# The left-over-token loop between the loads and the products of the last expert half, and a final norm from row sums

## The chip, the core and the metric

The kernel runs on one core of one Trainium2 chip. The metric is device time in microseconds (us). Three runs of the kernel before took 2152.41, 2152.41 and 2153.8 us; their median is 2152.41 us. One further execution was profiled, and every row below comes from that one.

Names used here: PE is TensorE (PEld its weight loads), DVE is VectorE, ACT is ScalarE, POOL is GpSimd, SP is SyncE, which in this kernel mostly issues DMAs. All tensors are float32.

## What is computed

Two layers of a diffusion block over 256 latent tokens and 256 context tokens of width 1024. Each layer has three token mixers (attention, gated linear attention, neighbourhood attention) and then a mixture of experts. The second layer needs only the latent tokens behind its mixers, so its expert part has 256 tokens (two tiles of 128 rows) where the first layer's has 512 (four tiles). What this case touches is the end of each layer:

```
h2 = LN0(x) * (1 + scale2) + shift2
x  = LayerNorm(alpha * x + gate2 * HierMoE(h2))   # top-1 group, then top-2 experts in it

def layer_norm0(x):
    mu  = x.mean(-1)
    var = square(x - mu).mean(-1)
    return (x - mu) * rsqrt(var + 1e-6)
def layer_norm(x, g, b): return layer_norm0(x) * g + b

def expert_block(xb, e):          # blocks of 128 token slots, 32 experts
    return (silu(xb @ w1[e]) * (xb @ w3[e])) @ w2[e]      # 1024 -> 512 -> 1024
```

The next layer begins with `h = LN0(x) * (1 + scale1) + shift1` and one wide projection of h.

## The kernel before

**Experts.** `experts(l, T)` walks over "halves": pieces of 128 token slots that belong to one, two or four experts, 14 halves in layer 0 and 16 in layer 1. The last half of each layer holds two experts with 64 slots each. One expert's weights are six tiles of 1 MB: w1 (j = 0, 1), w3 (j = 2, 3), w2 (j = 4, 5). So a half of two experts needs eight tiles for `body` (the products h = x·w1 and x·w3, 32 matmuls in two PSUM tiles) and four for `tail` (the SwiGLU `act`, four transposes, and the products Y = act·w2 in two column halves of 512, each split into a high and a low part Yh and Yl for the exact scatter). `body(n)` runs ahead of `tail(n-1)`. After every second half, `combine` scatters the Y of two halves back to the token tiles: products `cb` with a selection matrix C, a multiplication with the gate row (`ct`, L1432), and an addition to x (L1433), on POOL or, for the second column half of the last pair, on DVE.

**Loads.** SP issues every weight load in program order (L1464 and, for halves of a tile, L1469). A load waits until the buffer that it will fill is free. The buffers are rings: `ew` with six tiles in both layers, `ewb`, and in layer 1 some `spare` tiles made of areas that the mixers had used. Once the rings are full, a load starts when the products on the tile that lay there are done.

**The loop.** Slots beyond what the halves hold are done by `overflow(l, T)`: a device loop `For_i` (L1546) over a number of blocks that is read from a tile at run time (`values_load`, L1545). With these inputs the number is zero; no instruction of the loop's body is in the trace. The loop stands behind the last `tail`. At a loop the five engines meet: each runs a short block of semaphore waits, branches, and goes on in the code behind the loop. Those waits are the EVENT_SEMAPHORE records of L1546.

**The final norm.** Before, it reads statistics with `bn_stats` (L336, one record for 512 columns) and `bn_aggr` (L338), makes the inverse root by a chain of ten short DVE instructions (L340 to L346) on several token tiles at once, and applies it. In layer 0 ACT scales (L1597), DVE multiplies with g (L1598), and POOL or DVE adds b (L1599); in layer 1 two DVE steps (L1590, L1593) do it, and SP stores the result (L1595). g and b (`lgb`) are two rows broadcast to 512 KB each (L1612).

**Layer 1's start.** Behind layer 0's loop come the loads of the modulation weights (`wmod`, 16 of 512 KB, L493), the products on them (`tmod`, L495), the store of two x tiles to memory (L1601), the norm that opens the layer (`norm_T`: statistics, `xh` on ACT at L539, transposes `hT` at L550), and the wide projection in exact three-pass products (L380 to L382).

**What sets the order.** Each engine runs its instructions in the order of the program, which the scheduler of the tile framework makes from the code's order with priorities; waits are semaphores between engines. DMAs are queued in the order in which SP or ACT issues them.

Of the kernel before, what the change touches and what calls it, by code (L numbers as in the profile page):

```python
# [10 lines left out]
F32 = mybir.dt.float32  # L11
# [238 lines left out]
class _Prog:  # L250
# [281 lines left out]
    def norm_T(self, l, xs):  # L532
# [3 lines left out]
        for a in range(0, 4, NT[l]):  # L536
            for t, (_, r, m) in enumerate(self.stats_all(xs[a:a + NT[l]], APN[l]), a):
                h = self.t([128, 1024], ("whi", "wlo")[t % 2] if l else "g4", name="xh")
                nc.scalar.activation(h, xs[t], AF.Identity, bias=m, scale=r)  # L539
                xh.append(h)  # L540
# [858 lines left out]
    def expert_tail(self, h1, h3, gate, w2, halves, end=False):  # L1399
# [20 lines left out]
    def combine(self, CY, T, last):  # L1420

        nc, mm = self.nc, self.nc.tensor.matmul
        for n in range(2):
            for t in range(T):
# [8 lines left out]
                (nc.vector if last and n else nc.gpsimd).tensor_tensor(self.x1[t][:, ns], self.x1[t][:, ns], tmp, op=ALU.add)  # L1433
# [10 lines left out]
    def load(self, l, us, n, js, step=2048, most=99, after=None):  # L1444
# [4 lines left out]
        for j in js:  # L1449
            for i in range(len(us)):  # L1450
# [7 lines left out]
                if n < 6 or n >= 6 + extra:  # L1458
# [4 lines left out]
                    for v in range(0, 2048, step):  # L1463
                        self.nc.sync.dma_start(x[:, v:v + step], src[:, v:v + step])  # L1464
# [7 lines left out]
    def experts(self, l, T):  # L1472
# [39 lines left out]
        def tail(dp, pr, us, hs):  # L1512
            end = SPL and 2 * dp + pr == len(halves) - 1
            self.load(l, us, 2 * dp + pr, (4,))
            self.load(l, us, 2 * dp + pr, (5,), 1024 if end else 2048)
            w = self.held[2 * dp + pr]
            Y = self.expert_tail(hs[0], hs[1], gates[dp][:, pr:pr + 1],
                                 lambda f, n, i: w[i, 4 + n][f], len(us), end)
# [8 lines left out]
        for n, x in enumerate(halves):  # L1527
            if x[1] == 1 and x[0] + 1 < len(gs):
                front(x[0] + 1)
            with self.later(0 if n else FIRST):  # L1530
                held[n] = body(*x)
            if n:
                tail(*halves[n - 1], held[n - 1])
        tail(*halves[-1], held[len(halves) - 1])
    def overflow(self, l, T):

# [4 lines left out]
        nc.vector.tensor_scalar(idx0, idx0, c["pcol"][:, 0:1], 6.0, op0=ALU.add, op1=ALU.mult)  # L1541
        if l:
            nc.vector.tensor_scalar(idx0, idx0, float(l * NE * 768), None, op0=ALU.add)
        table = self.a["ew"].rearrange("l e p j w -> (l e p j) w")
        nblk = nc.values_load(self.nblk[0:1, 0:1], min_val=0, max_val=16)  # L1545
        with self.tc.For_i(0, nblk, 1):  # L1546
# [3 lines left out]
            w = []  # L1550
            for j in range(6):
                ii = self.small(1, I32)
                nc.vector.tensor_scalar(ii, row, float(j), None, op0=ALU.add)
                x = self.t([128, 2048], "ew", name="ow")
                nc.gpsimd.indirect_dma_start(out=x, out_offset=None, in_=table, in_offset=bass.IndirectOffsetOnAxis(ap=ii[:, :1], axis=0))
                w.append(x)
# [10 lines left out]
            for m in range(2):  # L1567
                h = self.ps("h")
                for k in range(8):
                    mm(h, XT[:, k], w[2 * m + k // 4][:, 512 * (k % 4):512 * (k % 4) + 512], start=k == 0, stop=k == 7)  # L1570
                hs.append(h)
            Y = self.expert_tail(hs[0], hs[1], gate, lambda f, n, i: w[4 + n][:, 512 * f:512 * f + 512], 1)
            col = self.small(1)
            nc.vector.tensor_tensor(col, sel, c["pcol"][:, 0:1], op=ALU.add)
            self.combine([(self.spots(self.slot_rows(self.over, T), col, T),) + Y], T, False)
# [5 lines left out]
    def final_norm(self, l, T, lgb):  # L1581

        nc = self.nc
        x = self.x1
        g, b = lgb
        for a in range(0, T, NB[l]):
            ts = range(a, a + NB[l])
            for t, (mu, r, m) in zip(ts, self.stats_all([x[t] for t in ts], APF[l])):
                if t in FQ[l]:
                    nc.vector.scalar_tensor_tensor(x[t], x[t], mu, g, op0=ALU.subtract, op1=ALU.mult)  # L1590
                    for i in range(2):
                        s = slice(512 * i, 512 * i + 512)
# [119 lines left out]
```

## Time and profile before

| what | value |
|---|---|
| median of three runs | 2152.41 us |
| the profiled execution | 2150.77 us |
| its span (first to last instruction) | 2148.9 us |
| outside the span | 1.9 us |
| PE busy in the span | 1973.0 us, 92% |
| DVE, ACT, POOL busy | 964.7, 561.5, 277.5 us |
| moved by DMA | 562.41 MB, mean 262 GB/s |
| mean granted TensorE clock | 0.969 |

The span is one axis of time from 0 to 2148.9 us: layer 0's mixers, its experts (until about 1194), layer 1's mixers, its experts, and the final norm. PE is busy in nearly all of it, but a busy PE in the expert parts can be a PE that is paced by weights: the products follow the stream of tiles. [...]

### The profile page before, as it was taken

To read this page: it belongs to the slowest core of one execution; us is meant where nothing else is said; L and a number is where in the kernel's file an instruction comes from. 1 tells how busy PE (TensorE), PEld (TensorE's weight loads), DVE (VectorE), ACT (ScalarE), POOL (GpSimd) and SP (SyncE) were. 2 spreads that over 40 slices of the span, in tenths; PEclk is the share of its full clock that TensorE was granted. 3 is DMA by queue.
4 is the path that set the end of the run, shared out by engine and by line. 5 is a ranking of instruction groups with operands and counts; after the bars stand their busy time and mean duration, and the time that the engine had idled before them with its cause. 6 is when DMAs were issued, how large, how long until landed. Compare 5 with 4: busy or idle time off the path is not lost. (4 is left out here: it accounts for less than half of the span.)

```text
span 2148.9 us, 28075 instructions
## 1 busy us (share of the span) xinstructions
PE 1973.0 (92%) x10749; PEld 1179.0 (55%) x10749; DVE 964.7 (45%) x2236; ACT 561.5 (26%) x992; POOL 277.5 (13%) x268
## 2 busy tenths in 40 slices
PE   6999999999998898989899598999996999999995
PEld 2676777767885353445253176887795433333331
DVE  4676765554487131222022766776658222221113
ACT  3453344443333000000010254444452111100000
POOL 1322100011100010111011222100020001000000
PEclk9999999999999999999999798999997999999998
DMA  8436222333328999999998723642466999999995
GB/s 300 160 118 220 69 69 70 94 99 120 99 91 321 400 420 420 372 385 420 420 369 367 276 84 116 197 127 85 140 210 253 401 421 422 422 422 422 421 422 224
DMA packets 113987, 562.41 MB, mean 262 GB/s; under 512 B 13302, under 2 KB 14838, under 8 KB 72120
## 3 DMA queue, kind: packets, MB, share of 16 engines
q1 hardware_dynamic: 113272, 558.85, 67.7%
q8 instruction: 87, 1.43, 0.3%
q10 hardware_dynamic: 576, 1.70, 0.2%
q14 instruction: 52, 0.43, 0.1%
HBM read 557.36 MB, written 3.15 MB: 261 GB/s over the span
## 5 line engine op out<-in xcount | busy, mean ns | idle before, releaser
L1507 PE MATMUL h<-ew,XT 128*64 128x512 f32 (+2 forms) x2048 | 479.0, 616 | 39.6 <-DMA ew<-in_ew_dram 39.5
L1507 PEld LDWEIGHTS h<-ew,XT 128*64 128x64 f32 (+2 forms) x2048 | 147.3, 136 | 325.7 <-issue 251.0
L1415 PE MATMUL Y<-ew,aT 128*64 128x512 f32 (+2 forms) x1024 | 250.4, 598 | 10.2 <-DMA ew<-in_ew_dram 7.8
L292 DVE TENSOR_TENSOR wlo<-raw,whi 128x1024 fp32r<-128x1024 f32 (+1 forms) x140 | 179.1, 1279 | 138.0 <-ACT whi L291 136.9
L1433 POOL TENSOR_TENSOR x<-x,ct 128x512 f32<-128x512 f32 x82 | 104.9, 1306 | 996.9 <-DVE ct L1432 873.7
L380 PE MATMUL pT<-hThi,whi 128*128 128x512 f32 (+1 forms) x576 | 204.0, 354 | 2.2 <-DVE zq L869 1.4
L291 ACT CAST whi<-raw 128x1024 fp32r<-128x1024 f32 (+1 forms) x140 | 145.4, 1039 | 223.4 <-PE pT L381 123.8
L382 PE MATMUL pT<-hThi,wlo 128*128 128x512 f32 (+1 forms) x576 | 203.2, 353 | 0.2 <-DVE wlo L292 0.2
L381 PE MATMUL pT<-hTlo,whi 128*128 128x512 f32 (+1 forms) x576 | 202.9, 352 | 0.0
L1404 DVE SCALAR_TENSOR_TENSOR act<-h,s,sl 128x512 f32<-128x512 f32 x30 | 22.5, 751 | 317.6 <-PE h L1507 263.9
L806 ACT CAST Yh<-Y 128x512 fp32r<-128x512 f32 x60 | 35.2, 586 | 467.7 <-PE Y L1415 467.7
L1415 PEld LDWEIGHTS Y<-ew,aT 128*64 128x64 f32 (+2 forms) x1024 | 75.5, 133 | 149.2 <-issue 123.8
L807 DVE TENSOR_TENSOR Yl<-Y,Yh 128x512 fp32r<-128x512 f32 x60 | 41.4, 690 | 252.8 <-ACT Yh L806 249.7
L380 PEld LDWEIGHTS pT<-hThi,whi 128*128 128x128 f32 x576 | 110.7, 192 | 23.8 <-issue 6.0
L382 PEld LDWEIGHTS pT<-hThi,wlo 128*128 128x128 f32 x576 | 110.7, 192 | 16.1 <-issue 2.6
L381 PEld LDWEIGHTS pT<-hTlo,whi 128*128 128x128 f32 x576 | 110.7, 192 | 14.3 <-issue 1.9
L380 PE MATMUL pM<-whi,hThi 128*128 128x512 f32 (+1 forms) x304 | 110.7, 369 | 3.6 <-ACT qTkT L645 1.9
L381 PE MATMUL pM<-wlo,hThi 128*128 128x512 f32 (+1 forms) x304 | 110.9, 365 | 0.0
L382 PE MATMUL pM<-whi,hTlo 128*128 128x512 f32 (+1 forms) x304 | 110.1, 364 | 0.0
L495 PE MATMUL mod<-wmod,sT 128*32 128x512 f32 x320 | 75.2, 636 | 22.5 <-DVE s L341 14.1
L1408 ACT COPY aT<-aT 128x512 f32<-128x512 f32 x30 | 17.6, 585 | 294.4 <-PE aT L1407 294.4
L1384 PE MATMUL XT<-OH,h2hi 128*128 128x256 f32 x352 | 88.6, 289 | 0.2 <-DVE OH L1362 0.2
(364 smaller groups left out, 3088.5 us busy)
## 6 DMA issues: line engine op xcount, KB each, us to landing
ew<-in_ew_dram SPq DMA_DIRECT2D x326, 1024.0 KB, 13.6
raw<-in_w_dram SPq DMA_DIRECT2D x145, 512.0 KB, 3.7
ew<-in_ew_dram SPq DMA_DIRECT2D x116, 512.0 KB, 13.5
wmod<-in_wmod_dram SPq DMA_DIRECT2D x96, 512.0 KB, 6.4
nb<-in_nb_dram SPq DMA_DIRECT2D x32, 256.0 KB, 3.8
g<-md SPq DMA_DIRECT2D x12, 256.0 KB, 7.3
row<-in_ln_dram SPq DMA_DIRECT2D x4, 512.0 KB, 5.3
lgb<-in_ln_dram SPq DMA_DIRECT2D x4, 512.0 KB, 12.2
```

Source lines behind the costliest of these rows:

```text
L291: self.nc.scalar.copy(hi, src)
L292: (eng or self.nc.vector).tensor_tensor(lo, src, hi.bitcast(F32), op=ALU.subtract)
L380: mm(out, lh, rh, start=start, stop=False)
L381: mm(out, lh, rl, start=False, stop=False)
L382: mm(out, ll, rh, start=False, stop=stop)
L495: nc.tensor.matmul(p[32 * j:32 * j + 32, :], self.sT[:, k, :], raws[j // 2][:, 512 * (j % 2):512 * (j % 2) + 512], start=k == 0, stop=k == 7)
L806: self.nc.scalar.copy(hi, src)
L807: self.nc.vector.tensor_tensor(lo, src, hi.bitcast(F32), op=ALU.subtract)
L1384: mm(p[:, w * j:w * j + w], self.h2s[t][part][:, 128 * k:128 * k + 128], OH[:, t], start=t == 0 and part == 0, stop=t == T - 1 and part == 1)
L1415: mm(y[m * i:m * i + m, :], aT[:, 128 * f + m * i:128 * f + m * i + m], w2(f, n, i), start=f == 0, stop=f == 3)
L1433: (nc.vector if last and n else nc.gpsimd).tensor_tensor(self.x1[t][:, ns], self.x1[t][:, ns], tmp, op=ALU.add)
L1507: mm(h[m * i:m * i + m, :], XTs[dp][:, k, 128 * pr + m * i:128 * pr + m * i + m], w[i, 2 * q + k // 4][k % 4], start=k == 0, stop=k == 7)
```

## The change

Five things change.

1. For the last half of each layer, `tail(n-1)` comes first, then the loads of the last half's eight w1 and w3 tiles, then the loop `overflow`, and only then `body` with the last half's 32 products, and its `tail`.
2. The loop's body gathers its weights in pieces of 512 columns, in the `ct` buffers, and so needs no `ew` buffer.
3. The last half's w2 is loaded behind the loop, all of it in halves of 1024 columns, the two experts taking turns, and into `ew` buffers. The loads of g and b (`final_loads`) stand ahead of them, in both layers. The Y products of the last half lose the order that took one expert after the other.
4. `combine` of the last pair makes its addition with an instruction that also gives the row sum, on DVE for both column halves. The final norm takes the mean from these sums, the variance from an ACT Square with a row sum, an inverse root for each token tile by itself, and two DVE steps, in both layers. In layer 0 the second one gives row sums again, and layer 1's `norm_T` takes its mean from those and its variance from ACT.
5. The final norm of layer 0 stands ahead of the opening of layer 1's buffers (`mixers(1)`).

The core of the diff:

```diff
 def expert_tail(...):
-            order = [(f, i) for f in range(4) for i in range(halves)]
-            for f, i in sorted(order, key=lambda x: x[1]) if end else order:
+            for f, i in [(f, i) for f in range(4) for i in range(halves)]:
 def combine(self, CY, T, last):
+        if last:
+            self.sums = [self.small(2) for _ in range(T)]
-                (nc.vector if last and n else nc.gpsimd).tensor_tensor(self.x1[t][:, ns], self.x1[t][:, ns], tmp, op=ALU.add)
+                if last:
+                    nc.vector.scalar_tensor_tensor(self.x1[t][:, ns], tmp, 1.0, self.x1[t][:, ns], op0=ALU.mult, op1=ALU.add, accum_out=self.sums[t][:, n:n + 1])
+                else:
+                    nc.gpsimd.tensor_tensor(self.x1[t][:, ns], self.x1[t][:, ns], tmp, op=ALU.add)
 def load(...):
         for j in js:
+            if step < 2048:
+                xs = [self.t([128, 2048], "ew", name="ew") for _ in us]
+                self.nw += len(us)
+                for v in range(0, 2048, step):
+                    for i, x in enumerate(xs):
+                        self.nc.sync.dma_start(x[:, v:v + step], w["src"][i][:, j, v:v + step])
 def tail(dp, pr, us, hs):
-            end = SPL and 2 * dp + pr == len(halves) - 1
-            self.load(l, us, 2 * dp + pr, (4,))
-            self.load(l, us, 2 * dp + pr, (5,), 1024 if end else 2048)
+            end = 2 * dp + pr == len(halves) - 1
+            self.load(l, us, 2 * dp + pr, (4, 5), 1024 if end else 2048)
 def experts(...):
-            with self.later(0 if n else FIRST):
-                held[n] = body(*x)
-            if n:
+            if n == len(halves) - 1:
                 tail(*halves[n - 1], held[n - 1])
+                self.load(l, x[2], n, range(4))
+                self.overflow(l, T)
+            held[n] = body(*x)
+            if 0 < n < len(halves) - 1:
+                tail(*halves[n - 1], held[n - 1])
+        lgb = self.final_loads(l)
         tail(*halves[-1], held[len(halves) - 1])
+        return lgb
 def final_norm(self, l, T, lgb):
-            for t, (mu, r, m) in zip(ts, self.stats_all([x[t] for t in ts], APF[l])):
...
+        for t in range(T):
+            nc.vector.tensor_scalar(nmu, self.sums[t][:, 0:1], self.sums[t][:, 1:2], -1.0 / 1024, op0=ALU.add, op1=ALU.mult)
+            nc.scalar.activation(junk[:, t % 2], x, AF.Square, bias=nmu, accum_out=v)
+            nc.vector.tensor_scalar(v, v, 1.0 / 1024, EPS, op0=ALU.mult, op1=ALU.add)
+            r = self.rsqrt(v, 1, st[:, 3:6])
+            STT(x, x, nmu, g, op0=ALU.add, op1=ALU.mult)
+            if l == NL - 1:
+                for i in range(2):
+                    STT(x[:, s], x[:, s], r, b[:, s], op0=ALU.mult, op1=ALU.add)
+                    nc.sync.dma_start(self.out[0, 128 * t:128 * t + 128, s], x[:, s])
+                continue
+            STT(x, x, r, b, op0=ALU.mult, op1=ALU.add, accum_out=st[:, 6:7])
+            if t < 2:
+                nc.sync.dma_start(self.x2[t], x)
 def run(self):
-            self.experts(l, T)
-            if l:
-                lgb = self.final_loads(l)
-            self.overflow(l, T)
+            lgb = self.experts(l, T)
+            xs = self.final_norm(l, T, lgb)
             if l == 0:
                 right.close()
                 left.close()
                 self.pre.close()
                 left, right = self.mixers(1)
-                lgb = self.final_loads(l)
-            xs = self.final_norm(l, T, lgb)
```

How the change moves instructions shows at three places. The rows are an engine's program order; `ew` with a number is one buffer of expert weights, `h` and `Y` are the two PSUM results, and the branches of L1546 (before) or L1577 (after) are the loop.

SP at the end of layer 1, before: the last half's w2 is issued in eight halves of 512 KB, and then comes the loop.

```order
L1464 DMA ew_15867<-in_ew_dram 128x2048
L1469 DMA ew_13686<-in_ew_dram 128x1024
L1469 DMA ew_13688<-in_ew_dram 128x1024
L1469 DMA ew_13691<-in_ew_dram 128x1024
L1469 DMA ew_13693<-in_ew_dram 128x1024
L1546 COMPARE_AND_BRANCH
L1546 UNCONDITIONAL_BRANCH x2
L1546 REGISTER_ALU
L1595 DMA out_dram<-x_2650_13358 128x512 x2
```

The same place after: the last full tile is one of the last half's w3; g and b and all of w2 stand behind the loop.

```order
L1488 DMA ew_15955<-in_ew_dram 128x2048
L1488 DMA ew_15957<-in_ew_dram 128x2048
L1577 COMPARE_AND_BRANCH
L1577 UNCONDITIONAL_BRANCH x2
L1577 REGISTER_ALU
L1649 DMA lgb_16254<-in_ln_dram 128x1024 x2
L1471 DMA ew_16257<-in_ew_dram 128x1024
L1471 DMA ew_16258<-in_ew_dram 128x1024
L1471 DMA ew_16263<-in_ew_dram 128x1024
L1471 DMA ew_16264<-in_ew_dram 128x1024
L1636 DMA out_dram<-x_2687_13443 128x512 x2
```

Two 512 KB loads and all eight halves of w2 moved from ahead of the loop to behind it.

PE at the end of layer 1, before: the last scatter products `cb` stand ahead of the loop, and behind it nothing but the program's end.

```order
L1430 MATMUL cb_15971<-Yl_15928,C_15952 128x512
L1430 MATMUL cb_15979<-Yl_15928,C_15952 128x512
L1545 TENSOR_LOAD r_4_13668
L1546 COMPARE_AND_BRANCH
L1546 REGISTER_ALU
L1546 UNCONDITIONAL_BRANCH
L1708 UNCONDITIONAL_BRANCH
```

After: the Y products of the half before the last stand ahead of the loop, and the last half's h products behind it.

```order
L1424 MATMUL Y_15928<-ew_15900,aT_15906 64x512
L1424 MATMUL Y_15928<-ew_15902,aT_15906 64x512
L1576 TENSOR_LOAD r_4_13753
L1577 COMPARE_AND_BRANCH
L1577 REGISTER_ALU
L1531 MATMUL h_16220<-ew_15943,XT_15618 64x512
L1531 MATMUL h_16220<-ew_15945,XT_15618 64x512
```

The 32 h products, the transposes, the 16 Y products and the last scatter moved from ahead of the loop to behind it; layer 0 shows the same.

SP at the start of layer 1, before: the 16 modulation loads start right behind the loop, and the two stores of x (`x_0`, `x_1`, memory tiles) stand among them.

```order
L1546 UNCONDITIONAL_BRANCH
L1612 DMA lgb_9055<-in_ln_dram 128x1024
L493 DMA wmod_9242<-in_wmod_dram 128x1024
L493 DMA wmod_9267<-in_wmod_dram 128x1024
L493 DMA wmod_9275<-in_wmod_dram 128x1024
L1601 DMA x_0_77<-x_1063_5264 128x1024
L493 DMA wmod_9283<-in_wmod_dram 128x1024
L1601 DMA x_1_78<-x_1077_5383 128x1024
L493 DMA wmod_9299<-in_wmod_dram 128x1024
```

After: all 16 stand behind both stores, which wait for the final norm.

```order
L1471 DMA ew_9002<-in_ew_dram 128x1024
L583 DMA cs_9413<-in_cst_dram 128x256
L595 DMA wg_9427<-in_wg_dram 33x512
L1641 DMA x_0_77<-x_1063_5264 128x1024
L1641 DMA x_1_78<-x_1077_5383 128x1024
L493 DMA wmod_9327<-in_wmod_dram 128x1024
L493 DMA wmod_9328<-in_wmod_dram 128x1024
```

The first modulation load moved from ahead of the final norm to behind two of its four tiles. On PE, ten of the 16 groups of `tmod` products stood ahead of the first transpose `hT` before; after, two do, and the other 14 stand among the transposes and the first products of the projection.

## Rows read from the trace of the kernel before

**Rows 1.** Page, parts 1 and 5: engine or group, count | busy, mean | idle, releaser.
```profile
PE 1973.0 (92%) x10749; PEld 1179.0 (55%) x10749; DVE 964.7 (45%) x2236; ACT 561.5 (26%) x992; POOL 277.5 (13%) x268
L1507 PE MATMUL h<-ew,XT 128*64 128x512 f32 (+2 forms) x2048 | 479.0, 616 | 39.6 <-DMA ew<-in_ew_dram 39.5
```

**Rows 2.** Windows at both layers' ends: busy of each engine, PEclk, DMA share, GB/s.
```profile
1164.00:1168.00 4.00, 4.00 (x21) 1.18 (x17) 0.75 (x1) 0.00 (x0) 0.00 (x0) 1.00 1.01 420
1172.00:1176.00 4.00, 4.00 (x19) 1.41 (x17) 1.35 (x2) 0.59 (x1) 0.00 (x0) 1.00 0.81 323
1176.00:1180.00 4.00, 3.38 (x16) 1.36 (x13) 0.59 (x1) 0.58 (x1) 0.00 (x0) 1.00 0.03 10
...
2120.00:2124.00 4.00, 4.00 (x17) 1.09 (x17) 0.00 (x0) 0.00 (x0) 0.00 (x0) 1.00 0.39 158
```

**Rows 3.** The loop's line L1546 on PE: ns min/median/max, starts; who waited behind it.
```profile
L1546 PEldq EVENT_SEMAPHORE  x25: 51/51/2622, 1189.5 to 2134.5; - x25
...
  DVE s L336: 3.3, 2
```

**Rows 4.** Timeline of layer 1's end: start, us, engine, line, operation, count [idle before].
```profile
2107.49 0.75 DVE L1404 SCALAR_TENSOR_TENSOR act<-h,s,sl 128x512 f32<-128x512 f32 x1 [17.80 <-PE h L1507]
2108.71 3.65 PE L1415 MATMUL Y<-ew,aT 128*64 128x512 f32 x16 [1.32 <-DMA ew<-in_ew_dram]
2112.29 0.66 PE L1407 MATMUL aT<-cst,act 128*128 128x128 f32 x4
2122.20 1.94 PE L1415 MATMUL Y<-ew,aT 128*64 128x512 f32 x8
2129.90 0.58 ACT L806 CAST Yh<-Y 128x512 fp32r<-128x512 f32 x1 [5.14 <-PE Y L1415]
2130.54 0.73 PE L1429 MATMUL cb<-Yh,C 128*128 128x512 f32 x2 [0.68 <-ACTq L1546]
2136.07 2.47 DVE L336 BATCH_NORM_STATS2 s<-x 128x6 f32<-128x512 f32 x4 [1.70 <-issue]
2138.70 1.27 DVE L1590 SCALAR_TENSOR_TENSOR x<-x,s,lgb 128x1024 f32<-128x1024 f32 x1
2143.21 2.73 DVE L1593 SCALAR_TENSOR_TENSOR x<-x,s,lgb 128x512 f32<-128x512 f32 x4
```

**Rows 5.** Timeline from layer 0's end into layer 1's opening.
```profile
1186.00 0.59 ACT L806 CAST Yh<-Y 128x512 fp32r<-128x512 f32 x1 [6.62 <-PE Y L1415]
1195.34 4.84 DVE L336 BATCH_NORM_STATS2 s<-x 128x6 f32<-128x512 f32 x8 [1.62 <-issue]
1204.07 1.92 PE L495 MATMUL tmod<-wmod,sT 128*32 128x512 f32 x4 [14.64 <-DMA raw<-in_w_dram]
1206.15 9.86 POOL L1599 TENSOR_TENSOR x<-x,lgb 128x1024 f32<-128x1024 f32 x3 [19.43 <-DMA raw<-in_w_dram]
1224.36 4.64 ACT L539 ACTIVATE xh<-x,s 128x1024 f32<-128x1024 f32 x4 [16.15 <-DVE s L346]
1231.10 1.05 PE L495 MATMUL tmod<-wmod,sT 128*32 128x512 f32 x4
```

**Rows 6.** Timeline of PE in layer 1's mixers, behind another pause.
```profile
1641.10 1.97 PE L1151 MATMUL h2T<-cst,h 128*128 128x128 f32 x8 [10.92 <-ACT h L320]
```

**Rows 7.** Windows behind the two pauses of PE and in layer 1's opening, columns as in Rows 2.
```profile
1200.00:1215.00 15.00, 9.61 (x30) 1.33 (x32) 13.63 (x38) 4.64 (x4) 8.85 (x3) 0.65 1.03 407
1230.00:1250.00 20.00, 17.87 (x76) 7.22 (x74) 10.26 (x15) 12.33 (x21) 6.03 (x4) 0.93 0.32 112
...
1641.00:1651.00 10.00, 9.49 (x44) 9.15 (x44) 6.20 (x22) 7.04 (x13) 0.00 (x0) 0.51 1.01 386
```

**Rows 8.** Single lines, ns min/median/max: ACT Square with row sum, DVE step with row sum.
```profile
L312 ACT ACTIVATE h<-x,s x1: 1133/1133/1133, 641.1 to 641.1; 128x1024 f32<-128x1024 f32 x1
L312 ACT ACTIVATION_READ_ACCUMULATOR h<-x,s x1: 185/185/185, 642.1 to 642.1; 128x1 f32 x1
...
L355 DVE SCALAR_TENSOR_TENSOR x<-u,s,row x6: 1277/1285/1286, 616.2 to 1639.7; 128x1024 f32<-128x1024 f32 x6
```

More of the change, by code (lines that the diff above doesn't have):

```diff
@@ L535, in norm_T @@
         xh = []
-        for a in range(0, 4, NT[l]):
+        for t in range(4 if l else 0):
+            h, st = self.t([128, 1024], ("whi", "wlo")[t % 2], name="xh"), self.small(20)
+            nmu, v, m = (st[:, i:i + 1] for i in range(3))
+            nc.vector.tensor_scalar(nmu, self.total[t], -1.0 / 1024, None, op0=ALU.mult)
+            nc.scalar.activation(h, xs[t], AF.Square, bias=nmu, accum_out=v)
+            nc.vector.tensor_scalar(v, v, 1.0 / 1024, EPS, op0=ALU.mult, op1=ALU.add)
+            r = self.rsqrt(v, 1, st[:, 3:6])
+            nc.vector.tensor_tensor(m, nmu, r, op=ALU.mult)
+            nc.scalar.activation(h, xs[t], AF.Identity, bias=m, scale=r)
+            xh.append(h)
+        for a in range(0, 0 if l else 4, NT[l]):
             for t, (_, r, m) in enumerate(self.stats_all(xs[a:a + NT[l]], APN[l]), a):
-                h = self.t([128, 1024], ("whi", "wlo")[t % 2] if l else "g4", name="xh")
+                h = self.t([128, 1024], "g4", name="xh")
                 nc.scalar.activation(h, xs[t], AF.Identity, bias=m, scale=r)
@@ L1397, in spots, with expert_tail @@
         return C
-    def expert_tail(self, h1, h3, gate, w2, halves, end=False):
+    def expert_tail(self, h1, h3, gate, w2, halves):
         nc, mm = self.nc, self.nc.tensor.matmul
@@ L1462, in load @@
                         self.nc.gpsimd.tensor_copy(x[0:32, 0:1], after[0:32, 0:1])
-                    for v in range(0, 2048, step):
-                        self.nc.sync.dma_start(x[:, v:v + step], src[:, v:v + step])
+                    self.nc.sync.dma_start(x, src)
                     w[i, j] = [x[:, 512 * v:512 * v + 512] for v in range(4)]
@@ L1549, in overflow, with piece @@
             nc.vector.scalar_tensor_tensor(eq, eq, 1.0, idx0, op0=ALU.mult, op1=ALU.mult, accum_out=row)
-            w = []
-            for j in range(6):
+            def piece(j):
                 ii = self.small(1, I32)
                 nc.vector.tensor_scalar(ii, row, float(j), None, op0=ALU.add)
-                x = self.t([128, 2048], "ew", name="ow")
+                x = self.t([128, 512], "ct", name="ow")
                 nc.gpsimd.indirect_dma_start(out=x, out_offset=None, in_=table, in_offset=bass.IndirectOffsetOnAxis(ap=ii[:, :1], axis=0))
-                w.append(x)
+                return x
             d = self.small(2 * T)
@@ L1569, in overflow @@
                 for k in range(8):
-                    mm(h, XT[:, k], w[2 * m + k // 4][:, 512 * (k % 4):512 * (k % 4) + 512], start=k == 0, stop=k == 7)
+                    mm(h, XT[:, k], piece(8 * m + k), start=k == 0, stop=k == 7)
                 hs.append(h)
[L1572 to L1575, printed above, removed]
+            Y = self.expert_tail(hs[0], hs[1], gate, lambda f, n, i: piece(16 + 4 * n + f), 1)
+            p = self.ps("row")
+            for t in range(T):
+                nc.tensor.transpose(p[:, 128 * t:128 * t + 128], OH[:, t].bitcast(F32), self.ident)
+            C = self.t([128, 128 * T], "o1", F32R, "C")
+            nc.vector.tensor_copy(C, p[:, :128 * T])
+            self.combine([(C,) + Y], T, False)
             nc.vector.tensor_scalar(cnt, cnt, 1.0, None, op0=ALU.add)
@@ L1583, in final_norm @@
         nc = self.nc
[L1584 removed]
+        STT = nc.vector.scalar_tensor_tensor
         g, b = lgb
[L1586 to L1601 removed]
@@ L1604, in final_loads @@
+        return self.x1
     def final_loads(self, l):
         nc = self.nc
-        if l:
-            x = self.t([128, 2, 1024], "e8", name="lgb")
-            lgb = [x[:, 0], x[:, 1]]
-        else:
-            lgb = [self.t([128, 1024], "g4", name="lgb") for _ in range(2)]
+        x = self.t([128, 2, 1024], "e8", name="lgb")
+        lgb = [x[:, 0], x[:, 1]]
         for i in range(2):
```

31 lines of the change are left out of this document (16 added, 15 removed).

## The prediction

> **What bounds the kernel now.** The page says that PE is busy 92% of the span, and that its largest group, the h products, sits idle 39.6 us in all, nearly all of it for weights [rows 1]. So most of the expert part is a stream of weights with products that keep up. The windows show that stream at 420 GB/s and a full DMA share until shortly before each layer ends [rows 2]: a tile of 1 MB (1.05 million bytes) takes 2.5 us. In layer 0 the stream is over at about 1176 (share 0.81 up to 1176, 0.03 behind it), in layer 1 at about 2122: the last window has 158 GB/s for 4 us, 0.63 MB or 1.5 us, and the products on the last pieces begin at 2122.20 [rows 2, 4]. From there on nothing is loaded, and the end is a chain: Y, its split, the scatter, the additions, the loop, the norm.
>
> What the loop costs now is small: the first instruction behind it on DVE, the statistics, waits 1.62 and 1.70 us, 3.3 us in all [rows 3 to 5], and nothing is in flight there. But line L1546 also shows what kind of thing the loop is: PE has 25 semaphore waits for two executions, one of them 2.6 us long [rows 3]. In the program these waits name every other engine and every lane of the DMA queues. So an engine gets past the loop only when all that was issued before it has landed. This is the row on which I decide, since the change puts the loop where the stream is at its fullest.
>
> **The loop's new place.** Ahead of it now lie the last half's eight w1 and w3 tiles; behind it lie the last half's 32 products, its w2, and the tail. Before, the products on the first tiles began while the last tiles were still coming. Now no product begins until the eighth tile has landed.
>
> When does it land? The ring and the order of what comes before it are the same but for the four w2 tiles of the half before, which now go first; so the eighth tile lands when the whole stream would, less what was moved behind the loop. Layer 1: four tiles of w2 and 1 MB of g and b, 5.24 MB at 420 GB/s, 12.5 us: 2122 − 12.5 = 2109.5. Layer 0, whose g and b already stood behind the loop: 4.19 MB, 10.0 us, 1176 − 10 = 1166. The waits and branches add about 1 us (half of the 1.6 to 1.7 us that DVE shows [rows 4, 5]; bounds 0.5 and 1.7). PE restarts at B = 1167 and 2110.5.
>
> From B the path is PE's. A run of 16 products takes 3.65 us, 0.215 each [rows 4]. Sixty-four records of h: 13.8 us. The scatter of the half before among them, 8 cb at 0.25 (a pair takes 0.73 with its tail [rows 4]): 2.0. Then act 0.75, transposes 0.66 [rows 4], a copy of 512 columns on ACT (as long as the Yh cast, 0.58 [rows 4]) and the gaps between them, 2.45 together. Y for the first 512 columns 3.65, for the second 3.65 and 1.0 for the scatter between. Sum 26.55 at full clock; in layer 0, whose four token tiles double the scatter, 1.5 more.
>
> PE will have been idle before B: the Y products ahead of the loop are done about when their w2 has landed, eight tiles (20 us) earlier, plus their own length and PE's lag, so it sits still for some 8 to 15 us. [...]
>
> [...]
>
> The last Yh cast then begins at 2110.5 + 26.55 + 3.2 = 2140.3 in layer 1, against 2129.90 [rows 4]: **+10.4**. In layer 0 at 1167 + 28.05 + 3.2 = 1198.3 against 1186.00 [rows 5]: **+12.3**.
>
> w2 itself starts only at B, and each piece waits until PE has read the w1 or w3 tile in its `ew` buffer. g and b and the first two tiles need 3.1 MB, 7.5 us, and are wanted 18 us after B or later; the last two wait for the end of the h products, about B + 18, need 5 us, and are wanted from about B + 25. That hides with 2 us to spare: cost 0, bounds 0 and 3 per layer.
>
> **The new final norm in layer 1.** From that cast to the last DVE step it takes 16.04 us now (2129.90 to 2145.94 [rows 4]). Out go the gap of 1.70 and the statistics, 2.47 and 0.24 for the aggregation up to the next step at 2138.70: 4.34 us. In come a mean, about 0.3, an ACT Square of 1.13 + 0.19 [rows 8] and one short step, 1.8 to 1.9 together. The chain of short steps for the inverse root is now one per token tile, two interleaved; I take it as equal in length (bounds −0.5 and +1). The two DVE steps per tile stay. Saving 2.4, bounds 1.2 and 3.1. **Layer 1 in sum: +8.0.**
>
> **The new final norm in layer 0.** From the last Yh cast to the end of the last `xh` (1224.36 + 4.64) it takes 43.0 us now [rows 5]. In it: the gap 1.62, statistics 4.84, an inverse root for all four tiles, three additions of 3.3 us each on POOL [rows 5], and a second set of statistics. After: the scatter and additions up to the loop's old place, 7.7 us (1186.0 to 1193.7), then DVE work for four tiles. Per tile two steps of 1.28 with a row sum [rows 8] and ten short ones, about 1.6: 4.2 us, 16.8 in all; ACT's Squares run beside that. Behind the last tile a Square of 1.3, an inverse root of 1.5 and `xh` of 1.16: 4. Sum 28.5 to 30. Saving **13.5**, bounds 11 and 16.
>
> **Layer 1's opening.** The 16 `wmod` loads were issued from the loop on, and ten of the 16 groups of `tmod` products ran while PE waited for the norm. Now SP holds all 16 behind the two x stores, which wait for the second tile's final norm, at about 1198.3 + 7.7 + 8.4 = 1214.4; SP has nothing else to issue, so everything behind them is late, the projection's weights too. Eight groups of 1.05 us [rows 5] move from the idle PE into the stretch where PE is busy: the window 1230 to 1250 has PE busy 17.87 of 20 us [rows 7], so 2.1 us of holes can take some. Cost 8.4 − 2.1 = 6.3, taken as 6; bounds 2 (they fill waits between transposes) and 9 (and the first projection products wait for raw weights queued behind 8.4 MB, 20 us of stream). **Layer 0 with the opening: 12.3 − 13.5 + 6 = +4.8.** The loop's body does not run, so its smaller gathers cost nothing but code.
>
> Sum: 8.0 + 4.8 = +12.8 on the profiled execution, 2150.77 + 12.8 = 2163.6. The median of the runs is 1.6 above that execution, so the forecast is **2165 us**.
>
> **Rivals.**
>
> First, not slower: the loop does not expose the loads, because the engines wait only for their own tiles. Then the stream runs on, the last h products start as early as before, and what is left is the gain of the norms, −2.4 in layer 1 and −13.5 + 6 in layer 0. That is −9.9: 2142. The short waits of L1546 on most engines speak for it, since now they cost little; but there nothing is in flight [rows 2], and PE's one wait of 2.6 us [rows 3] and the program's waits on all lanes speak against it. It decides if PE's first h product behind the loop starts before the eighth tile has landed.
>
> [...]
>
> Second, about the same: the exposure is real but smaller. The clock does not fall (−6.4), the short norm chains save their upper bound (−3), and `tmod` hides in holes (−4), of which about 9 come together: +4, 2156.
>
> Third, dearer: clock at 0.51 for ten microseconds in both layers (+3.4), w2 late for Y (+3 in each layer), projection weights late (+3). That is +12 on top if all hold, 2177.
>
> **How the numbers follow.** A chance of 0.60 for the forecast (2160 to 2170), 0.17 for the second rival (2152 to 2160), 0.15 for the third (2170 to 2178), 0.08 for the first. The range 2155 to 2177 leaves out the first rival, a third of the second, and the tip of the third. A measurement of this kernel can tell about 0.2%, 4.3 us, from no change. Faster by more: 0.07, nearly all of the first rival. Within: 0.10, the lower part of the second. Slower: 0.83.
>
> **What would show it.** In the trace of after, PE should stand still for 8 to 15 us ahead of the loop in each layer, start h at about 1167 at half clock, and the DMA engines should pause for about a microsecond at the loop and then load w2 while h runs. In layer 1 layer 0's 4.8 come on top, so h starts there at about 2115. The last Yh should come near 1198 and 2145, and the end of the last DVE step 13.6 us behind the latter. The first `wmod` issue should follow the second x store. I am wrong if PE runs through the loop, if the last `xh` does not come about 13 us sooner behind Yh, or if the products at the start of layer 1 have no holes left and wait for weights.

## The result, and the profile after

The changed kernel took 2166.97 us (median of five runs, 2163.22 to 2169.73) against 2152.41 us for the kernel before. The ratio is 1.0066 with a 95% interval of 1.0052 to 1.0081: slower by 14.6 us, clear of the 0.2% that a measurement can tell. The forecast was 2165 us. The profiled execution of the changed kernel took 2169.31 us, span 2167.5 us.

The two profiled executions are 18.5 us apart, more than the medians. 2.9 us of that lie ahead of everything that was changed: the first h product of layer 0's experts starts at 692.51 before and at 695.41 after. So times are compared from marks inside the program. Five serve for all runs: A, the first h product of layer 0's experts; B, the end of layer 0's last scatter product; C, the first z product of layer 1 (its opening is done); D, the first h2T product (layer 1's mixers are done); E, the end of the span. They are read from PE's timeline of each run.

| run | A to B | B to C | C to D | D to E | median, us |
|---|---|---|---|---|---|
| before | 496.9 | 57.9 | 393.8 | 507.8 | 2152.4 |
| after | 510.7 | 44.9 | 397.8 | 518.7 | 2167.0 |
| e1, loop last | 499.4 | 48.3 | 399.2 | 506.6 | 2147.9 |
| e2, no loop | 501.9 | 44.4 | 399.6 | 509.1 | 2145.4 |
| e3, as after | 513.5 | 44.9 | 396.2 | 520.0 | 2166.2 |
| e4, norm alone | 497.6 | 48.1 | 389.0 | 509.0 | 2136.9 |
| e5, none ahead | 516.1 | 45.2 | 395.9 | 513.3 | 2162.4 |
| e6, four ahead | 502.7 | 45.4 | 400.5 | 507.3 | 2147.6 |
| e7, early opening | 513.8 | 46.5 | 391.7 | 516.9 | 2161.9 |
| e8, two steps | 496.7 | 53.8 | 390.0 | 509.5 | 2145.7 |
| e9, mixed | 497.7 | 47.0 | 388.2 | 508.7 | 2135.0 |
| e10, e4 again | 499.0 | 48.8 | 388.7 | 509.6 | 2138.1 |

The runs were made in rounds on several chips, with the kernel before timed again in each: 2150.7 us beside e1 to e4, 2152.5 beside e5 to e8, 2152.1 beside e9 and e10. The ratios below are to that. Two kernels were profiled twice, after (with e3) and e4 (with e10); between the two executions A to B differs by 2.8 and 1.5 us, each other stretch by at most 1.6.

Before to after: +13.8 at the end of layer 0, −12.9 in the norm and the opening, +4.0 in layer 1's mixers, +10.9 in layer 1's experts and end; +15.7 in all.

On the page the h products have nearly the same busy time as before (477.9 us for 479.0) and 24.6 us more idle time ahead of them [rows 1]:

```profile
L1531 PE MATMUL h<-ew,XT 128*64 128x512 f32 (+2 forms) x2048 | 477.9, 613 | 64.2 <-DMA ew<-in_ew_dram 53.3
```

The timeline of layer 0's end shows one half of it (start, length, engine, what, count, idle before):

```profile
1170.73 6.22 PE L1531 MATMUL h<-ew,XT 128*64 128x512 f32 x16 [10.78 <-DVE cnt L1570]
...
1203.20 0.59 ACT L816 CAST Yh<-Y 128x512 fp32r<-128x512 f32 x1 [7.17 <-PE Y L1424]
...
1220.46 1.91 SPq L1641 DMA_DIRECT2D x<-x  x2
...
1222.41 13.55 SPq L493 DMA_DIRECT2D wmod<-in_wmod_dram  x10
...
1229.98 3.50 ACT L544 ACTIVATE xh<-x,s 128x1024 f32<-128x1024 f32 x3
```

PE stood still for 10.78 us at the loop and then took 6.22 us for 16 products, 3.65 at full clock [rows 4]. The releaser that the row names, a memset on DVE behind the loop, was merely the last to report; every engine had been waiting for the loads, SP for 9.2 us until the last tile had landed at 1169.5. Behind it, the last Yh cast is at 1203.20 where it was at 1186.00 [rows 5], and the modulation loads start only behind both x stores. The timeline of layer 1's end shows the other half:

```profile
2121.62 5.23 PE L1531 MATMUL h<-ew,XT 128*64 128x512 f32 x16 [17.09 <-DMA ew<-in_ew_dram]
...
2151.21 0.59 ACT L816 CAST Yh<-Y 128x512 fp32r<-128x512 f32 x1 [5.32 <-PE Y L1424]
...
2155.54 0.33 DVE L1627 TENSOR_SCALAR s<-s 128x1 f32<-128x1 f32 x2
...
2162.97 1.41 DVE L1635 SCALAR_TENSOR_TENSOR x<-x,s,lgb 128x512 f32<-128x512 f32 x2
```

Here PE waited 17.09 us. In both layers it went on at half clock: the granted clock, third number from the end with 1.00 as full speed, is 0.51 in the window from 1172 to 1176 and 0.50 in that from 2120 to 2124 (windows as in Rows 2).

```profile
1172.00:1176.00 4.00, 4.00 (x12) 1.04 (x10) 0.00 (x0) 0.00 (x0) 0.00 (x0) 0.51 0.64 208
2120.00:2124.00 4.00, 2.38 (x6) 0.77 (x8) 0.00 (x0) 0.00 (x0) 0.00 (x0) 0.50 0.44 101
```

The norm's first step follows the last addition at once, with no gap where 1.70 us stood [rows 4], and the last DVE step ends 13.17 us behind the Yh cast (it was 16.04).

What SP waited for at the loop, in the view of waits from 2100 to 2125 (what, in total, times, longest), and the DMA engines from 2085 to 2125 in 40 slices of one microsecond:

```profile
SPq L1577 <- DMA ew<-in_ew_dram: 17.8, 4, 10.5
```

```profile
DMA  9999999999999999999999999999999754100899
GB/s 410 430 414 422 414 422 414 438 410 430 438 426 434 434 410 426 442 401 426 410 426 434 410 418 393 426 410 418 418 418 401 311 238 188 66 0 0 233 172 356
```

SP passed four waits, one for each of the last four tiles (the trace has them at 2113.32, 2115.80, 2118.27 and 2120.75, a tile's 2.5 us apart). The stream is full until 2116, then runs out over four microseconds, and stands still until g and b are issued behind the loop at 2121.27.

### The profile page after: what moved, and what is told of

The parts are those of the page before. It is cut to its first block, busy times and chain, and to the rows that moved or that the text cites. A ratio compares the mean times of both kernels' runs of the same rounds, so it can differ in the third digit from the quotient of the medians.

```text
span 2167.5 us, 28131 instructions
## 1 busy us (share of the span) xinstructions
PE 1966.8 (91%) x10749; PEld 1173.1 (54%) x10749; DVE 961.3 (44%) x2275; ACT 568.8 (26%) x1008; POOL 260.8 (12%) x259
## 4 chain that ended last, share of the span: by engine, by line
PE 70%; DMA 19%; DVE 5%; ACT 3%; issue 1%; POOL 1%; SPq 0%; DVEq 0%; ACTq 0%; POOLq 0%
DMA ew<-in_ew_dram 16%; PE h L1531 14%; PE Y L1424 8%; PE pT L380 5%; PE pT L382 5%; PE pT L381 4%; PE XT L1394 3%; PE pM L380 2%; PE pM L381 2%; PE pM L382 2%; DMA wmod<-in_wmod_dram 2%; PE PV L969 2%; PE cb L1440 2%; PE mod L495 2%; PE cb L1441 2%; PE br L380 1%
## 5 line engine op out<-in xcount | busy, mean ns | idle before, releaser
L1531 PE MATMUL h<-ew,XT 128*64 128x512 f32 (+2 forms) x2048 | 477.9, 613 | 64.2 <-DMA ew<-in_ew_dram 53.3
L1448 POOL TENSOR_TENSOR x<-x,ct 128x512 f32<-128x512 f32 x76 | 97.3, 1306 | 938.8 <-DVE ct L1443 814.2
L816 ACT CAST Yh<-Y 128x512 fp32r<-128x512 f32 x60 | 35.2, 587 | 452.8 <-PE Y L1424 452.8
```

Of the source, the lines that this page charges most:

```text
L1448: nc.gpsimd.tensor_tensor(self.x1[t][:, ns], self.x1[t][:, ns], tmp, op=ALU.add)
L1531: mm(h[m * i:m * i + m, :], XTs[dp][:, k, 128 * pr + m * i:128 * pr + m * i + m], w[i, 2 * q + k // 4][k % 4], start=k == 0, stop=k == 7)
```

## The experiments

Two theories stood against each other from the start. Theory 1: at the loop every engine waits for every load issued, and this standing still is the loss. Theory 2: the new order of the last half's loads is the loss, w2 coming last and into buffers that the h products must free first.

**e1, the loop back behind the last tail.**

```diff
                 self.load(l, x[2], n, range(4))
-                self.overflow(l, T)
...
         tail(*halves[-1], held[len(halves) - 1])
+        self.overflow(l, T)
         return lgb
...
-            self.combine([(C,) + Y], T, False)
+            self.combine([(C,) + Y], T, True, False)   # renews the row sums
```

> Only the loop moves, from between the last half's loads and its products back behind the last tail; loads, w2 buffers, norm and layer 1's opening stay as in the changed kernel (the loop's own additions then renew the row sums). Theory 1, the wait: the changed kernel loses what PE stands still until the eighth tile has landed. The last Yh casts were 17.2 us (layer 0) and 13.5 us (layer 1) late; both go back, 30.7 us, and two gaps of 1.7 us at the loop come in: 2167 - 27 = 2140 us, PE idle behind the last half's loads gone. Theory 2, the order: w2 comes last, into buffers that the h products must free first, and this makes the end late; the loop itself costs 1.7 us wherever it stands: 2162 to 2170 us.

Measured: 2147.87 us, 0.9978 of the kernel before (0.9964 to 0.9992). Against the changed kernel the medians are 19.1 us apart, and A to E of the two profiles 18.6: that is what the loop's place alone is worth. A to B fell by 11.3 us and D to E by 12.1; the last load of w2 stayed where the change put it. In layer 1 the last half's products again follow the stream, with PE waiting a microsecond for a tile and not 17 for eight (PE's timeline of e1):

```profile
2111.78 3.65 PE L1531 MATMUL h<-ew,XT 128*64 128x512 f32 x16 [0.71 <-DMA ew<-in_ew_dram]
2116.80 3.65 PE L1531 MATMUL h<-ew,XT 128*64 128x512 f32 x14 [1.37 <-DMA ew<-in_ew_dram]
```

Theory 2 falls. But 2140 was expected, and 8 us are missing. That is an error of the expectation: its 17.2 us for layer 0 hold the 2.9 us by which that execution was late already, and the last Yh cast is no good mark between these two, since in e1 the casts of the last half are 3.4 us apart, with the scatter of both behind them, and 7.8 us in the changed kernel. By the marks A to E the loop's place costs 11.3 + 12.1 us, and 3.4 come back in B to C, where the gap behind the loop is gone. Against e4, the norm alone, which is 14 us faster than before, e1 loses 11.0 us, and 10.2 of them in C to D (399.2 against 389.0); e7 takes that up.

**e2, no loop at all.** The call is left out.

> The changed kernel without the loop (leaves out the blocks of left-over slots, of which these inputs have none). Theory 1: as with the loop last, less its two gaps of 1.7 us: 2136 us. Theory 2: 2160 to 2167 us. The difference to the run with the loop last is the loop's cost where nothing is in flight, 3 to 4 us.

Measured: 2145.43 us (0.9964, 0.9949 to 0.998), 2.4 us less than e1; the two intervals overlap, so this difference alone is not clear of the noise. The profiles point the same way. The stretches that hold the loop in e1 are shorter without it: from layer 0's last Yh cast to its last `xh` 35.2 us, not 38.4, and from layer 1's last Yh cast to the last DVE step 14.26, not 14.99. So a loop that runs no time, with nothing in flight, costs a microsecond or a few a layer here; in the kernel before the gaps behind it were 1.62 and 1.70 us [rows 4, 5].

**e3, meant to have the loop ahead of the loads.** The line that loads ahead of the loop was left out, so that `body` makes these loads, behind the loop in the code.

> The loop stays ahead of the last half's products, but goes ahead of its eight loads too. Theory 1 in full: a loop with nothing issued ahead of it that the products could already use costs only a pause of the stream. The stream of 12 tiles restarts 3 to 4 us late (drain and waits) and the products follow it tile by tile as in the kernel before, so the last Yh is 4 to 6 us late in each layer and not 17.2 and 13.5: 2167 - 20 = 2147 us (2143 to 2152). Theory 2: as the changed kernel, 2162 to 2170 us. Rival 3, the more loads stand behind the loop the more is exposed (20 us of stream in each layer): 2195 us or more.

Measured: 2166.24 us. SP's program shows why: the scheduler issued the eight loads ahead of the loop all the same, since their buffers came free before it. It is the changed kernel again, and shows only that it repeats to within a microsecond.

**e4, the norm alone** in the kernel before: `combine`, `final_norm` and `norm_T` of the change, with the loop, the loads and the opening as they were.

> The kernel before with the new norm alone: row sums in the last additions, variance on ACT, two DVE steps, row sums handed to layer 1's first norm; the loop last, the loads, buffers and layer 1's opening as before (modulation loads right behind the loop). Working from the changed kernel's trace: the norm saves 2.9 us in layer 1 and 12.7 us in layer 0 with the loop's gap counted; less the gaps of 1.7 and 1.6 that stay, 12.3 us: 2152.4 - 12.3 = 2140 us. Rival: in layer 1's opening the modulation loads (8.4 MB, until about 1222 in the kernel before) come before the transposes on PE, so that the earlier norm only waits for them and 5 to 6 us of the gain are lost: 2146 us. Rival 2, the norm gains nothing: 2152 us.

Measured: 2136.87 us, 0.9933 (0.991 to 0.9956); a second time 2138.10, 0.9935 (0.9922 to 0.9949). Each beside the kernel before of its own round, that is a gain of 13.9 and 14.0 us for the change's second part, and this version beats both kernels. Not all of it is seen where the norm works: by the marks, B to C gives 9.8 us, and layer 1's end from the last Yh cast to the last DVE step 0.7 (15.35 us for 16.04); 4.8 lie in C to D, where e4 changes nothing but what comes before (see e8). The rival, that the modulation loads take part of it back, is not seen: B to C fell by 9.8 us although PE still waited for them. In PE's timeline of e4 the first `tmod` group still waits for its load, at 1200.85 (1204.07 before [rows 5], 1.4 us earlier from A):

```profile
1200.85 1.92 PE L495 MATMUL tmod<-wmod,sT 128*32 128x512 f32 x4 [12.65 <-DMA wmod<-in_wmod_dram]
```

**e5 and e6, none and four of the eight loads ahead of the loop.** The loads behind it are held there by a copy on POOL that reads the loop's counter.

```diff
+                self.load(l, x[2], n, range(2))            # e6 alone: w1 ahead
-                self.load(l, x[2], n, range(4))
                 self.overflow(l, T)
+                self.load(l, x[2], n, range(4), after=self.cnt)
```

> The changed kernel with all eight w1 and w3 tiles of the last half behind the loop, held there by a copy of one column on POOL from the loop's counter into each tile (the run e3 was meant to do this, but the scheduler put the loads ahead of the loop again, so it was the changed kernel once more). Theory 1: SP gets past the loop once w2 of the half before has landed and its Y products are done, 16 us sooner than in the changed kernel in layer 1 (2105 on its axis, not 2121). Then 13 tiles stream behind it, 32.5 us, the products follow tile by tile, and the last Yh comes about 5 us behind the last piece: 2105 + 2.8 + 32.5 + 5 = 2145 instead of 2151, 5 to 6 us sooner in each layer: 2167 - 11 = 2156 us. Rival 3 (more loads behind the loop, more exposed): 2187 us or more, 10 us later in each layer. Theory 2 (order of w2): 2165 us.

> The same with the four w1 tiles ahead of the loop and the four w3 tiles behind it. Theory 1: the loop lets go when the fourth tile has landed, 9.9 us sooner than in the changed kernel; the products on w1 (7 us, partly at half clock) run while w3 streams, w3 is there 13 us behind the loop, and w2 as soon as it is wanted or 2 us late: last Yh about 9 us sooner in each layer: 2167 - 18 = 2149 us, sooner than with none ahead. Theory 2: 2165 us. Rival 3: between the changed kernel and the run with none ahead.

Measured: none ahead 2162.42 us, four ahead 2147.60 us, eight ahead (the change) 2166.97 us. Four ahead gives back all that the loop's place had cost, as much as e1: 19.4 us, where 18 were expected. PE's restart in e6, in layer 0 and in layer 1:

```profile
1159.10 5.28 PE L1533 MATMUL h<-ew,XT 128*64 128x512 f32 x16 [2.21 <-POOL ew L1487]
```

```profile
2101.79 4.97 PE L1533 MATMUL h<-ew,XT 128*64 128x512 f32 x16 [6.49 <-DMA ew<-in_ew_dram]
```

PE stands still for 2.21 and 6.49 us instead of 10.78 and 17.09, and while it works on w1 the w3 tiles arrive.

None ahead is the half miss. Layer 1 did as expected, D to E 5.3 us less than after. Layer 0 got 5.3 us worse. The DMA engines of e5 from 1130 to 1170, again a microsecond a slice:

```profile
DMA  9999999999993100000000000002969899999999
```

They stand still for 13 us. In layer 0 the products lag behind the loads. SP, with nothing more to issue ahead of the loop, waits there until PE has done the Y products that stand ahead of it too: the last of them ends at 1154.9, and SP's next load goes out at 1156.7. The windows show PE busy in the stretch where nothing is loaded, and its restart waits for the first tile (windows as in Rows 2; then PE's timeline):

```profile
1146.00:1150.00 4.00, 4.00 (x16) 1.29 (x12) 2.62 (x4) 0.59 (x1) 4.00 (x4) 1.00 0.00 0
1150.00:1154.00 4.00, 4.00 (x18) 1.69 (x18) 1.70 (x3) 0.00 (x0) 2.62 (x3) 1.00 0.00 0
```

```profile
1165.02 1.94 PE L1533 MATMUL h<-ew,XT 128*64 128x512 f32 x2 [5.81 <-DMA ew<-in_ew_dram]
```

So theory 1 was half of it. The loop holds both sides here: PE waits for the loads ahead of it (10.78 and 17.09 us in the changed kernel), and the loads behind it wait for PE (13 us without DMA in e5). Whichever was behind made the other stand still, and of the three numbers of loads ahead that were tried the middle one is best.

**e7, layer 1's buffers opened ahead of layer 0's norm,** in the changed kernel: `mixers(1)` and the loads of g and b stand where they stood, so that most modulation loads go ahead of the x stores.

> The changed kernel with layer 1's buffers opened ahead of layer 0's final norm again (g and b, and what ACT's Square writes, lie in other buffers for that): SP's program has 12 of 16 modulation loads ahead of the first x store. In the run with the loop last and in the changed kernel the stretch from the first z product to the first h2T product of layer 1's mixers took 399.2 and 397.8 us, in the kernel before 393.8 and with the norm alone 389.0. Theory: 4 to 6 us of the loss are this late opening: 2167 - 5 = 2162 us, and the first z product comes up to 3 us later, since more tmod products stand ahead of it. Rival: the opening is hidden, and that stretch differs by the clock's ups and downs alone: 2167 us.

Measured: 2161.90 us, 1.0047 of the kernel before (1.0033 to 1.0061). By the medians that is 5.1 us less than the changed kernel, as expected, by the two ratios 4, and their intervals overlap. The stretches are clearer: C to D 6.1 us less, B to C 1.6 more. And of all twelve profiles the six with the late opening take 395.9 to 400.5 us from C to D, the six with the early one 388.2 to 393.8. What the late opening costs is seen in PE's timeline of the changed kernel: six of the sixteen `tmod` groups, of 1.05 us each, stand behind C among the projection's products, the first and the last of them at

```profile
1256.54 1.05 PE L495 MATMUL tmod<-wmod,sT 128*32 128x512 f32 x4
...
1266.87 1.05 PE L495 MATMUL tmod<-wmod,sT 128*32 128x512 f32 x4
```

where PE has no holes.

**e8, layer 0's norm in two DVE steps, statistics as before:** `FQ = (0, 1, 2, 3), (0, 1)` for `(), (0, 1)` in the kernel before.

> The kernel before, with layer 0's final norm in two DVE steps per token tile as layer 1 has it, and its statistics as before (bn_stats, inverse roots of two tiles at once; no row sums, no ACT Square). It tells how much of the 13.9 us that the norm alone gives comes from the two steps in place of ACT, DVE and POOL, and how much from the row sums. If the three POOL additions of 3.3 us were what the end waited for: 2152 - 9 = 2143 us. If the statistics count, which DVE still makes twice (8 records of 0.6 us each time): DVE has 5 + 2.5 + 5.5 + 4.9 + 3 us behind the first aggregation, to about 1222 on the axis of before against 1224.4: 2149 us.

Measured: 2145.65 us, 0.9964 (0.9949 to 0.9978), between the two answers. In its timeline DVE is the chain, as the second answer has it: the two steps and then the second set of statistics, back to back.

```profile
1209.65 2.73 DVE L1593 SCALAR_TENSOR_TENSOR x<-x,s,lgb 128x512 f32<-128x512 f32 x4
1212.37 2.74 DVE L1593 SCALAR_TENSOR_TENSOR x<-x,s,lgb 128x512 f32<-128x512 f32 x4
1215.02 4.84 DVE L336 BATCH_NORM_STATS2 s<-x 128x6 f32<-128x512 f32 x8
```

B to C is 4.1 us shorter than before, where e4 has 9.8: of the norm's gain in layer 0 some four microseconds come from the two steps and six from the statistics that DVE no longer makes. Another 3.8 us lie in C to D, where nothing was changed. PE runs the same instructions there in the kernel before and in e8 and stands still for as long (23.8 and 23.7 us), but the same work takes it 369.98 us and 366.27 (windows from C to D of the two):

```profile
1247.30:1641.10 393.80, 369.98 (x2517) 302.82 (x2517) 258.95 (x583) 175.72 (x306) 59.25 (x82) 0.96 0.45 145
1244.75:1634.72 389.97, 366.27 (x2517) 300.08 (x2517) 258.78 (x583) 175.49 (x306) 60.18 (x82) 0.97 0.45 148
```

So it is the clock that differs. One of its falls can be followed. Of the kernel before and of e4 the z products at C, and the window from 1250 to 1270, read

```profile
1247.30 3.07 PE L619 MATMUL z<-aT,wg 33*128 33x512 f32 x4 [1.48 <-ACT aT L608]
1236.31 1.98 PE L629 MATMUL z<-aT,wg 33*128 33x512 f32 x4
```

```profile
1250.00:1270.00 20.00, 20.00 (x101) 17.47 (x101) 13.02 (x27) 12.90 (x15) 3.38 (x8) 0.88 0.19 53
```

```profile
1250.00:1270.00 20.00, 20.00 (x117) 16.84 (x116) 16.88 (x26) 11.88 (x17) 7.72 (x10) 1.00 0.40 124
```

In the kernel before PE waits 1.48 us for ACT ahead of C, and the clock is at half from 1248.05 to 1254.85: 0.88 in the window, though PE is busy in all of it. In e4 PE does not wait there, and the clock stays up. The other profiles agree but for one: where PE waited 1.05 to 1.49 us just ahead of C (before, e1, e2, e6, e7, e8) the clock fell within 3 us behind it; where it waited 0.51 us or not at all (after, e3, e4, e5, e10) it did not, nor in e9, where it waited 1.04. So the gain in C to D goes with the clock, and a part of that with this wait, which e4 does not have; the other falls between C and D were not followed.

**e9, mixed:** the norm and opening of e4; layer 0's loop last, layer 1's loop with four tiles ahead.

> The new norm in both layers with layer 1's early opening; layer 0 with its loads and the loop as in the kernel before (loop last), layer 1 with the loop behind the fourth tile of the last half, as in the run with four ahead. By the stages: from layer 0's first h product to the last scatter as with the norm alone (497.5 us), layer 1's mixers as there, and layer 1 from its first h2T product to the end 507.3 us as with four ahead and not 509.0: 1.7 us less than the norm alone, 2135 us. Rival: the stream's pause in layer 1 costs what the gap behind the loop gives back: 2137 us.

> The norm alone once more, beside the mixed kernel on the same chip: 2137 us (2134 to 2140).

Measured, side by side: e9 2134.95 us, 0.9917 (0.9903 to 0.993); e4's kernel again 2138.10 us. e9 has the lowest median, 17 us under the kernel before; its interval and that of e4's kernel still overlap at their edges. Its place is not as I said, though: D to E is 508.7 in the profile, 509.0 and 509.6 in the two executions of e4's kernel; the expected 1.7 us were not found there, and where the 3 us between the medians come from stays open.

## Why the prediction came out right, step by step

Times of after are set on the axis of before by taking off 2.9 us in layer 0; in layer 1 they are taken from mark D.

| step | forecast | measured |
|---|---|---|
| layer 0: PE restarts | 1167 | 1167.8 |
| clock at the restart | 3.2 lost | 2.6 (16 products in 6.22, not 3.65) |
| last Yh cast | +12.3 | +14.3 |
| Yh cast to the end of the last xh | −13.5 | −12.7 (30.3 for 43.0) |
| opening, tmod among busy products | +6 | +3.3 to D against before; in C to D 6.1 against e7 |
| layer 0 in sum | +4.8 | +4.9 |
| layer 1: PE restarts, from D | 469.4 | 472.8 |
| clock at the restart | 3.2 lost | 1.6 (5.23) |
| restart to the last Yh cast | 29.75 | 29.6 |
| last Yh cast | +10.4 | +13.5 |
| Yh cast to the last DVE step | −2.4 | −2.9 |
| layer 1 in sum | +8.0 | +10.7 |

The mechanism was the forecast's: the engines leave the loop only when the last load has landed (1169.5 and 2120.75), PE stands still (10.78 and 17.09 us), restarts at half clock (0.51 and 0.50), and the norm gives back part of it. e1 shows the loop's place to be worth 19 us, e4 shows the norm to be worth 14, e7 shows the late opening to be worth 4 to 5. These three make +9 to +10, not the +14.6 measured. Most of what is missing lies between e4 and e1: of their 10.2 us in C to D the six late `tmod` groups are 6.3 us, PE stands still 0.9 longer, and the rest goes with the clock (0.98 and 0.97).

The term that was off most is when the eighth tile lands. I had dated the end of the stream by its bytes at the full rate, and had put 1 us between that and PE's restart. In layer 1 it was 3.7 us: the last tile lands behind a tail of four microseconds at falling rate (2116 to 2120 above, 0.80 MB, worth 1.9 us at full rate). The waits and branches themselves took 0.87 us there (2120.75 to 2121.62) and 1.2 us in layer 0 (1169.5 to 1170.7), about what I had put. In layer 0 the last tile landed 1.9 us behind the end that its bytes give, but the bytes were through 1.3 us sooner than I had dated them, so that the restart came only 0.8 us late.

Part of the agreement is luck. Layer 0's +4.9 for +4.8 adds up misses of +2.0, +0.8 and −2.7 us. The last of these, the opening, holds the clock: between C and D the kernel before was granted 0.96 in its profile and the changed kernel 0.98, and without that the late opening would have cost more. In layer 1 the way from the restart to the last Yh cast took 29.6 us for 29.75 because 1.6 us less went to the clock and the work at full clock took 1.5 us more. And PE's pause there, 17.09 us, is longer than the 8 to 15 that I gave.

The clock at the restart cost less than I took. No run shows the 3.2 us that the sums hold for it in each layer; behind the loop it was 2.6 and 1.6 us: the first 16 products took 6.22 and 5.23 us, at a granted clock of 0.51 and 0.50 in the windows above, for 3.65 at full clock. As an estimate the term can be had from the kernel before, whose clock behind the pause of 14.64 us was 0.50 until 1210.5, 6.4 us from PE's restart at 1204.07 [rows 5]; half of that is 3.2 (windows as in Rows 2):

```profile
1200.00:1210.50 10.50, 5.80 (x16) 0.75 (x16) 9.13 (x35) 4.64 (x4) 4.35 (x2) 0.50 1.03 413
1210.50:1215.00 4.50, 3.81 (x18) 0.58 (x16) 4.50 (x4) 0.00 (x0) 4.50 (x2) 1.00 1.05 394
```

The third rival's +3.4 is the same estimate from ten microseconds at 0.51 [rows 7]: 4.9, or 1.7 more in each layer. The pauses were 10.78 and 17.09 us against 14.64 and 10.92 [rows 5, 6], and the longest had the smallest price, so the length of a pause alone did not set it.

The w2 loads behind the loop did cost nothing, as forecast: the first Y products behind the loop wait for ACT's copy in both layers (0.68 and 0.67 us). The first rival (engines wait only for their own tiles) is refuted: PE's first h product starts 0.87 us behind the landing of the eighth tile in layer 1, 1.2 us in layer 0. The third rival's late projection weights were not seen.

Two things were less simple than I had them. I thought of the loop as PE waiting for loads; e5 shows that loads wait for PE just as well (13 us without DMA in layer 0). And I had weighed only the eight loads of the change ahead of the loop; here four ahead (2147.6) beat eight (2167.0) as well as none (2162.4).

## What to carry to other kernels

The device loop was a meeting point for engines and DMA queues here, even though it ran no time: with eight tiles issued ahead of it PE stood still for 10.78 and 17.09 us. It cost least where nothing was in flight and no engine lagged (1.2 us each by the medians of e1 and e2, 3.2 and 0.7 in their profiles), so try it in such a place first, or split the loads around it: with four tiles ahead (2147.6 us for 2167.0) PE stood still for 2.21 and 6.49 us and had w1 to work on while w3 arrived. A change of two parts can hide a gain: here 14 us from the norm stood against 19 from the loop's place and 4 to 5 from a late opening, and one run of each part alone found it. When an end of a stream is dated, read when its last piece lands, not where the mean rate would end it (1.9 and 2.8 us apart here).

## What the runs showed of the hardware

The last tile of the stream ahead of the loop landed 2.8 us after the point at which its bytes would have ended at the full 420 GB/s in layer 1 (2117.9 and 2120.75), 1.9 us in layer 0 (1167.6 and 1169.5): in layer 1 the DMA rate fell over 311, 238, 188 and 66 GB/s in the last four microseconds. What makes it fall was not tried. The last four tiles still land 2.5 us apart, as in a running stream, so the lag is seen only at the end.

The granted clock fell to half (0.50) behind PE's long waits at the loop (10.78 and 17.09 us), and it fell too behind a wait of 1.48 us ahead of C in the kernel before, where the kernel with the norm alone had no wait and kept 1.00. The stretch C to D differs by up to 5.6 us between kernels that have nearly the same program there (388.2 to 393.8 us), but by 0.3 and 1.6 us between two executions of one kernel (389.0 and 388.7; 397.8 and 396.2). The kernel before was profiled once, so how much of its 393.8 us is that execution's own stays open; a difference of a few microseconds in one profile is better settled by the medians of five to ten runs.
